# Trunk kernel, two layers: folded mean and epsilon, two other banks for the first values, a shifted start of x's transposition, and a last group in halves

## The chip, the cores and the metric

The kernel runs on one core of a Trainium2 chip. The metric is the time of one execution on the device in microseconds (us). Before the change it is 1112.16 us, the median of three runs (1112.07 to 1112.44). All engine times below come from one execution that the hardware profiler recorded.

## What is computed

A trunk of two layers runs over 512 tokens of width 1024, in float32. Layer 0 is multi-head latent attention with 8 heads and a block-causal mask; layer 1 is chunked attention with 16 heads, a learned position bias and a shared key/value band made from layer 0's output. Each layer ends in a SwiGLU FFN with hidden width 2816. Every sub-layer is x + post_norm(f(pre_norm(x))), and the norm is the place that one part of the change touches:

```python
EPS = 1e-6
def rms_norm(x, g):
    xf = x.astype(jnp.float32)
    y = xf * lax.rsqrt(jnp.mean(xf * xf, axis=-1, keepdims=True) + EPS)
    return (y * g.astype(jnp.float32)).astype(x.dtype)

def swiglu(h, w_gate, w_up, w_down):
    return (jax.nn.silu(h @ w_gate) * (h @ w_up)) @ w_down

def reference(x, ...):
    for layer in range(DEPTH):
        h = rms_norm(x, attn_pre_g[layer])
...
        x = x + rms_norm(y, attn_post_g[layer])
        h = rms_norm(x, ffn_pre_g[layer])
        f = swiglu(h, ffn_w_gate[layer], ffn_w_up[layer], ffn_w_down[layer])
        x = x + rms_norm(f, ffn_post_g[layer])
        if layer == N_A_LAYERS - 1:
            k_band, v_band = shared_kv(x, kv_src_g, w_kv_shared)
    return x
```

## The kernel before

**Layout.** Activations mostly lie transposed: a tile is 128 features by 512 tokens, so a [512, 1024] activation is eight tiles. Weights stream from memory. Every float32 factor is split into a high and a low part (`whi` by a cast on ScalarE, L144; `wlo` by a subtraction on VectorE, L145), and every product is three matmuls on TensorE: high by high, low by high, high by low (`mm3`, L360 to L364). The FFNs use a scheme of sums and differences of blocks with fewer products than the plain one, whose partial sums are called `al`, `be`, `ga`, `de`.

**Order.** The code is written as generators whose steps are woven into each other; a scheduler then orders the instructions of each engine's queue by priorities (`first`, `behind` and `issue_after` shift them). Each engine runs its queue strictly in order. PSUM has banks of 128 x 512 in three groups: "mm" (four), "s" (two), "t" (two). A matmul group that takes a bank waits until the former contents have been read.

**Norms.** `Sum` (L423) squares each tile on ScalarE and adds the squares up on VectorE in `acc`. `total` (L444) transposes `acc` on TensorE (`tot`) and reduces it on VectorE into `ss` (L452). `rstd` (L455) multiplies by 1/n and adds epsilon on VectorE (`v`, L463), and takes the power -1/2 on GpSimd (`r`, L467). `spread` (L484) brings `r` back over the partitions by matmuls with an identity (`bc`). In layer 0 the latents are computed from an x that isn't normalised, so their norms use `rstd_of_scaled` (L470), which also needs the first norm's `r`.

**Values and rotary part of layer 0.** `values_a(c)` (L928) makes the values of four token tiles, for the heads' first half (c = 0) or second half (c = 1): one bank and six matmuls per token tile, then the split `va` (L145, from ScalarE's cast of the same name). `rotary(0)` (L942) makes the queries' rotary part in two "s" banks (b_617 and b_618 before, b_613 and b_614 after); VectorE combines them (`ra`, `rb`, L949 to L951) and splits them (`rl`). The queries' norm is `tot_600`, `ss`, `v`, `r` and `r2` in between (L473 to L477).

**FFN.** `ffn()` (L1083) computes the input norm while the first products run, then `products()` (L1469) makes the hidden tiles in nine pairs of seven blocks each, and `down()` (L1235) multiplies them by the down weights. In the second FFN, `by_tokens` (L1164) runs beside the products as `aside`: block by block it loads a part of x, transposes it on VectorE (`xt`, L1171) and writes it to the output by four transfers on the SP queue, so that x stands in the output by tokens. It takes 24 steps, three per pair.

**The end.** `AfterLast` (L1403) finishes the last FFN's output, which lies by tokens: for token tile i and output half o it adds up the partial sums (`y`, L1322), squares with accumulation (`sq`, `ss`, L1327), multiplies by the gain (`yg`, L1442), forms mean and epsilon (`ssv`, L1364 and L1365) and the power on GpSimd (`r`, L1368). `plus_x` (L1461) then multiplies by `r`, adds x and issues the write. The last block of `down` (E6) works in groups of weight tiles; the last group is (3, 4, 5), its first output (e = 0) belongs to token tile 2 and its second (e = 1) to tile 3.

Of the kernel before, what the change touches and what calls it, by code (L numbers as in the profile page):

```python
# [68 lines left out]
def trunk(ctx: ExitStack, tc: tile.TileContext, a, out):  # L69
# [353 lines left out]
    class Sum:  # L423


        def __init__(self, make=U):
            self.make, self.acc, self.begun = make, None, [False, False]

        def add(self, src, h=None):
# [4 lines left out]
            if not self.begun[h or 0]:  # L434
                ins = nc.scalar.activation(self.acc[:, c], src, AF.Square),
            else:
                q = self.make(name="sq")
                ins = (nc.scalar.activation(q[:, c], src, AF.Square),
                       V.tensor_tensor(self.acc[:, c], self.acc[:, c], q[:, c], op=OP.add))
            for i in ((0, 1) if h is None else (h,)):  # L440
                self.begun[i] = True
# [13 lines left out]
    def rstd(ss, n, eps=EPS):  # L455
        parts = ss if isinstance(ss, list) else [ss]
        m = sum(p.shape[1] for p in parts)
        v = small("v")[:, :m]
        w = m // len(parts)
        for i, p in enumerate(parts):  # L460
            o = v[:, i * w:(i + 1) * w]
            if eps is EPS:
                V.tensor_scalar(o, p, 1.0 / n, EPS, op0=OP.mult, op1=OP.add)  # L463
            else:
                V.scalar_tensor_tensor(o, p, 1.0 / n, eps[:, i * w:(i + 1) * w], op0=OP.mult, op1=OP.add)
        r = small("r")[:, :m]
        nc.gpsimd.tensor_tensor(r, v, mhalf[:, :m], op=OP.pow)  # L467
        return r

    def rstd_of_scaled(ss, n, r0):  # L470
# [4 lines left out]
        r = rstd(v, n)  # L475
# [92 lines left out]
    class Post:  # L568
        def __init__(self, gain, make=U, eps=None, op=OP.add):

            self.gain, self.make, self.sum, self.y, self.r = gain, make, Sum(make), [], {}
            self.eps, self.op = eps, op

        def rstd(self, ss, h):
            return rstd(ss, D, EPS if self.eps is None else self.eps[:, 2 * h:2 * h + 2])
# [17 lines left out]
        def add_half(self, h, banks, rest, n1, n2, end=None):  # L593
# [7 lines left out]
            with behind(end and at):  # L601
                ss = self.sum.total(h, 200)
            with first(200):
                r = self.rstd(ss, h)
# [4 lines left out]
        def finish(self, b):  # L609
# [3 lines left out]
            for src in (self.sum.acc, sq):  # L613
                if src is sq:
                    nc.scalar.activation(sq[:, HALF[1]], b[:, HALF[1]], AF.Square)
# [4 lines left out]
            self.r[1] = spread(self.rstd([i[:, :1] for i in t], 1), 2)  # L620
# [216 lines left out]
    skv = Sum()  # L837
# [8 lines left out]
    r0 = rstd(sx.total(), D)  # L846
# [59 lines left out]
    sq_ = Sum()  # L906
# [176 lines left out]
    def ffn(i, x_src, osp, firsts, late=()):  # L1083
# [44 lines left out]
        ss = sx.sum.total()  # L1128
# [666 lines left out]
```

## Time and profile before

| quantity | value |
|---|---|
| median of three runs | 1112.16 us |
| lowest to highest | 1112.07 to 1112.44 us |
| the profiled execution's own time | 1113.16 us |
| its span from the first to the last instruction | 1111.4 us |
| granted TensorE clock, mean | 0.998 |
| GpSimd busy | 68.3 us, 106 instructions |
| memory traffic | 118 GB/s over the span |

In the profile, PE is TensorE, DVE VectorE, ACT ScalarE, POOL GpSimd and SP the queue that issues most transfers. A row of a timeline gives the start in us, the duration in us, the engine, the line of the code, the operation, what is written and read by the program's names, the shapes and a count; in brackets stands how long the engine had been idle and what ended that wait. `PE ... b<-whi,ckh` is a matmul into bank b. Matmuls overlap: a 128 x 512 one takes 0.39 us from start to end, but the next starts 0.23 us later, so a stop is read from the starts. Neighbouring operations of the other engines overlap by a little less than 0.1 us as well.

### The profile page before, as it was taken

What the parts mean: (1) busy time and instruction counts of PE and PEld (TensorE: products, weight loads), DVE (VectorE), ACT (ScalarE), POOL (GpSimd) and SP (SyncE); (2) the same over time, 40 slices, a digit from 0 to 9 for tenths busy, and PEclk for the clock granted to TensorE, in tenths of its full rate; (3) what the DMA queues carried; (4) which work ended last, traced back from release to release, by engine and by line L of the source; (5) the groups of instructions that cost most, each with busy time, mean ns of one, the idle gap of its engine ahead of it and who ended that gap; (6) DMA issues with size and microseconds to landing.
All of it is one profiled execution on the core that took longest, in us unless ns stands there. A gap on an engine that the chain in (4) does not pass through costs nothing.

```text
span 1111.4 us, 18953 instructions
## 1 busy us (share of the span) xinstructions
PE 1098.7 (99%) x6941; PEld 980.9 (88%) x6941; DVE 936.2 (84%) x1679; ACT 682.5 (61%) x1331; POOL 68.3 (6%) x106
## 2 busy tenths in 40 slices
PE   9999999999999999999999999999999999999997
PEld 6888889999999998888888888889999999998885
DVE  7788737999989989978868887758999999989977
ACT  6476636755555556668635777657755555556675
POOL 1200000000000001400000000000000000002402
PEclk9999999999999999999999999999999999999999
DMA  7432216323232357961556565635334444558913
GB/s 238 113 111 77 77 63 222 134 63 110 95 133 96 108 183 236 157 198 40 190 152 170 142 175 151 169 97 189 134 104 123 132 137 124 150 192 244 173 29 76
DMA packets 79885, 152.93 MB, mean 138 GB/s; under 512 B 25328, under 2 KB 27120, under 8 KB 79792
## 3 DMA queue, kind: packets, MB, share of 16 engines
q1 hardware_dynamic: 72448, 138.71, 40.2%
q0 software_dynamic: 6912, 12.59, 6.9%
q8 instruction: 54, 0.88, 0.3%
q10 hardware_dynamic: 432, 0.44, 0.1%
q14 instruction: 39, 0.32, 0.1%
HBM read 120.56 MB, written 10.68 MB: 118 GB/s over the span
## 4 chain that ended last, share of the span: by engine, by line
PE 90%; DVE 5%; DMA 2%; issue 2%; ACT 1%; POOL 0%; DVEq 0%; POOLq 0%; SPq 0%; ACTq 0%
PE al L1499 17%; PE b L361 11%; PE b L362 11%; PE b L363 11%; PE be L1499 8%; PE al L1255 8%; PE be L1255 5%; PE ga L1499 4%; PE de L1255 3%; PE ga L1255 3%; PE pt L523 2%; DVE wlo L145 2%; DMA x<-in_x 1%; DMA raw<-in_w_pair 1%; PE b L1655 1%
## 5 line engine op out<-in xcount | busy, mean ns | idle before, releaser
L144 ACT CAST whi<-raw 128x1024 fp32r<-128x1024 f32 (+3 forms) x224 | 225.2, 1007 | 199.0 <-PE al L1499 65.1
L145 DVE TENSOR_TENSOR wlo<-raw,whi 128x1024 fp32r<-128x1024 f32 (+3 forms) x224 | 260.2, 1164 | 44.8 <-ACT whi L144 43.7
L1499 PE MATMUL al<-th,whi 128*128 128x256 f32 x432 | 122.9, 285 | 0.5 <-DVE ut L1511 0.5
L1499 PE MATMUL al<-th,wlo 128*128 128x256 f32 x432 | 121.0, 281 | 0.3 <-DVE wlo L145 0.3
L1499 PE MATMUL al<-tl,whi 128*128 128x256 f32 x432 | 120.9, 280 | 0.0
L361 PE MATMUL b<-xh,whi 128*128 128x512 f32 (+1 forms) x298 | 114.6, 386 | 0.4 <-ACT whi L144 0.4
L363 PE MATMUL b<-xh,wlo 128*128 128x512 f32 (+1 forms) x298 | 110.3, 370 | 0.3 <-DVE wlo L145 0.3
L362 PE MATMUL b<-xl,whi 128*128 128x512 f32 (+1 forms) x298 | 109.9, 369 | 0.0
L174 DVE TENSOR_TENSOR raw<-raw,raw 128x1024 f32<-128x1024 f32 x72 | 86.9, 1218 | 2.5 <-DMA raw<-in_w_pair 2.2
L1499 PEld LDWEIGHTS al<-th,whi 128*128 128x128 f32 x432 | 81.3, 188 | 2.8 <-DVE ut L1511 0.9
L1499 PEld LDWEIGHTS al<-th,wlo 128*128 128x128 f32 x432 | 81.2, 188 | 0.6 <-DVE wlo L145 0.5
L1499 PEld LDWEIGHTS al<-tl,whi 128*128 128x128 f32 x432 | 81.3, 188 | 0.0
L511 ACT ACTIVATE p<-p,mn 128x128 f32<-128x128 f32 (+1 forms) x96 | 54.0, 562 | 39.3 <-DVE mn L509 38.4
L145 DVE TENSOR_TENSOR ptl<-pt,pth 128x128 fp32r<-128x128 f32 (+1 forms) x96 | 46.6, 486 | 29.4 <-ACT pth L144 23.7
L145 DVE TENSOR_TENSOR wlo<-wd,whi 128x512 fp32r<-128x512 f32 x86 | 56.3, 685 | 14.7 <-ACT whi L144 14.4
L363 PEld LDWEIGHTS b<-xh,wlo 128*128 128x128 f32 x298 | 56.2, 189 | 10.8 <-DVE wlo L145 1.2
L144 ACT CAST whi<-wd 128x512 fp32r<-128x512 f32 x86 | 49.8, 618 | 25.0 <-PE al L1255 10.7
L361 PEld LDWEIGHTS b<-xh,whi 128*128 128x128 f32 x298 | 56.5, 189 | 6.7 <-ACT whi L144 0.9
L362 PEld LDWEIGHTS b<-xl,whi 128*128 128x128 f32 x298 | 56.5, 190 | 5.8 <-DVE xl L149 0.2
L144 ACT CAST pth<-pt 128x128 fp32r<-128x128 f32 (+1 forms) x96 | 40.3, 421 | 26.8 <-PE pt L523 26.0
L1255 PE MATMUL al<-whi,pl 128*128 128x512 f32 x132 | 51.5, 390 | 0.0
L1255 PE MATMUL al<-whi,ph 128*128 128x512 f32 x132 | 51.4, 389 | 0.0
(313 smaller groups left out, 3266.8 us busy)
## 6 DMA issues: line engine op xcount, KB each, us to landing
raw<-in_w_pair SPq DMA_DIRECT2D x72, 512.0 KB, 3.8
wd<-in_w_down SPq DMA_DIRECT2D x54, 256.0 KB, 5.8
raw<-in_w_o SPq DMA_DIRECT2D x16, 512.0 KB, 3.6
raw<-in_w_gu SPq DMA_DIRECT2D x16, 512.0 KB, 4.2
raw<-in_w_down SPq DMA_DIRECT2D x16, 512.0 KB, 4.3
raw<-in_w_qkb SPq DMA_DIRECT2D x16, 512.0 KB, 3.5
wd<-in_w_down POOLq DMA_DIRECT2D x22, 256.0 KB, 5.2
wd<-raw POOLq DMA_DIRECT2D x22, 256.0 KB, 4.6
```

Source lines behind the costliest of these rows:

```text
L144: return (nc.scalar.copy(dst_hi, src), V.tensor_tensor(dst_lo, src, dst_hi.bitcast(F32), op=OP.subtract))
L145: V.tensor_tensor(dst_lo, src, dst_hi.bitcast(F32), op=OP.subtract))
L174: V.tensor_tensor(t, x, y, op=OP.add)
L361: nc.tensor.matmul(o, l[0], r[0], start=start, stop=False)
L362: nc.tensor.matmul(o, l[0], r[1], start=False, stop=False)
L363: last_mm[0] = nc.tensor.matmul(o, l[1], r[0], start=False, stop=stop)
L511: nc.scalar.activation(p[:, :n], p[:, :n], AF.Exp, bias=mn[:, :1], scale=-1.0, accum_out=self.sums[:, qt:qt + 1])
L523: nc.tensor.transpose(t[:, kt * P:(kt + 1) * P], p[:, kt * P:(kt + 1) * P], ident)
L1255: nc.tensor.matmul(to[e], l[c], r[d], start=j < 4 and k == 0 and n == 0, stop=k == NF // 2 - 1 and n == 2, skip_group_check=True)
L1499: nc.tensor.matmul(o, l[c], r[d], start=first_ and n == 0, stop=k == K2 - 1 and n == 2, skip_group_check=True)
L1655: nc.tensor.matmul(o[:, q_], vv, ptl[:, kt, q_], start=False, stop=kt == NQT - 1)
```

## The change

It has four parts.

1. *Mean and epsilon.* The squares are made with a scale of D^-0.5, so the sum is the mean already; the first addition of squares adds EPS/128 to each partition's share, which makes epsilon in the sum over 128 partitions. `rstd` is then the power alone. The two latents' norms keep the old form (`mean=False`), with the operation moved into `rstd_of_scaled`.
2. *Banks.* Of the first values (c = 0), token tiles 0 and 3 take an "s" bank each.
3. *x.* In `products`, the `aside` steps begin with the second pair (p = 1).
4. *The last group.* For e = 1 the group (3, 4, 5) runs in two halves of 256 columns: the first onto the old bank, the second in a fresh one of group "t" (`last`). What the old bank already held in the second half is added to `y` earlier (in `during`). `half` handles each half; the write for (0, 2) is issued behind that for (1, 2).

```diff
     class Sum:
-        def __init__(self, make=U):
-            self.make, self.acc, self.begun = make, None, [False, False]
+        def __init__(self, make=U, mean=True):
+            self.make, self.acc, self.begun, self.eps = make, None, [False, False], [mean, mean]
+            self.scale = D ** -0.5 if mean else 1.0
...
+                ins = nc.scalar.activation(q[:, c], src, AF.Square, scale=self.scale),
+                if self.eps[both[0]]:
+                    ins += V.scalar_tensor_tensor(t, t, EPS / P, q[:, c], op0=OP.add, op1=OP.add),
+                    for i in both:
+                        self.eps[i] = False
+                else:
+                    ins += V.tensor_tensor(t, t, q[:, c], op=OP.add),
...
-    def rstd(ss, n, eps=EPS):
-        parts = ss if isinstance(ss, list) else [ss]
...
-                V.tensor_scalar(o, p, 1.0 / n, EPS, op0=OP.mult, op1=OP.add)
...
+    def rstd(v):
+        r = small("r")[:, :v.shape[1]]
+        nc.gpsimd.tensor_tensor(r, v, mhalf[:, :v.shape[1]], op=OP.pow)
         return r
...
-        r = rstd(v, n)
+        V.tensor_scalar(v, v, 1.0 / n, EPS, op0=OP.mult, op1=OP.add)
+        r = rstd(v)
...
-    skv = Sum()
+    skv = Sum(mean=False)
...
-    sq_ = Sum()
+    sq_ = Sum(mean=False)
...
-            b = bank()
+            b = bank() if c or tt % 3 else bank("s")
...
-        V.tensor_scalar(eps, ss, EPS / D, EPS * EPS, op0=OP.mult, op1=OP.add)
+        V.tensor_scalar(eps, v, EPS, None, op0=OP.mult)
...
+                end = group[-1] == Down.TILES - 1
                 for e in range(2):
...
+                    for o, cols in post.parts(j, e, to[e]) if end else ((to[e], ALL),):
+                        fresh = o is not to[e]
...
+                                    nc.tensor.matmul(o[:, cols], l[c], r[d], start=begin and n == 0,
...
+                        if cols is not ALL:
+                            post.half(o, cols)
+                        elif end:
+                            post.one(j, e, o)
+                post.during(j, group[0], to)
...
+            if j == Down.E6 and i == 2:
+                t, c = self.y[0][3], HALF[1]
+                V.tensor_tensor(t[:, c], t[:, c], banks[1][:, c], op=OP.add)
...
+        def parts(self, j, e, b):
+            if j != Down.E6 or not e:
+                return (b, ALL),
+            return (b, HALF[0]), (bank("t", "last"), HALF[1])
+
+        def half(self, b, c):
+
+            t, v, q = self.y[0][3], self.v[:, 3:4], HALF.index(c)
+            with first(200):
+                V.tensor_tensor(t[:, c], t[:, c], b[:, c], op=OP.add)
+                sq = U(name="sq")
+                nc.scalar.activation(sq[:, c], t[:, c], AF.Square, accum_out=self.ends[:, q:q + 1])
+                if not q:
+                    self.yg = U(name="yg")
+                    V.scalar_tensor_tensor(v, self.ss[1][:, 3:4], 1.0 / D, self.eps[:, 3:4], op0=OP.mult, op1=OP.add)
+                V.tensor_tensor(self.yg[:, c], t[:, c], self.g[0][:, c], op=OP.mult)
+                self.summed = V.scalar_tensor_tensor(v, self.ends[:, q:q + 1], 1.0 / D, v, op0=OP.mult, op1=OP.add)
+                if q:
+                    self.y[0][3] = self.yg
+                    self.r[3] = small("r")[:, :1]
+                    nc.gpsimd.tensor_tensor(self.r[3], v, mhalf[:, :1], op=OP.pow)
...
                 if i == 2:
                     self.plus_x(1, 2, nc.sync)
+                    self.plus_x(0, 2, nc.scalar)
...
             with tc.issue_after(self.summed.ins):
-                self.plus_x(0, 2, nc.scalar)
                 self.plus_x(1, 3, nc.sync)
...
-                if aside is not None and j in (1, 3, 5):
+                if aside is not None and p and j in (1, 3, 5):
                     next(aside, None)
```

The built programs show how the queues change. First VectorE in the first FFN's input norm, before and after (`wlo` is the low part of a weight, `acc` the sum of the output norm of the attention, `bc` the spread factor):

```order
L145 TENSOR_TENSOR wlo_2349<-raw_2209,whi_2348 128x1024
L439 TENSOR_TENSOR acc_1940<-acc_1940,sq_2078 128x256
L452 TENSOR_REDUCE ss_2115<-tot_2112 128x2
L145 TENSOR_TENSOR wlo_2388<-raw_2303,whi_2387 128x1024
L463 TENSOR_SCALAR v_2117<-ss_2115 128x2
L439 TENSOR_TENSOR acc_1940<-acc_1940,sq_2147 128x256
```
```order
L145 TENSOR_TENSOR wlo_2341<-raw_2203,whi_2340 128x1024
L447 TENSOR_TENSOR acc_1936<-acc_1936,sq_2074 128x256
L460 TENSOR_REDUCE ss_2111<-tot_2108 128x2
L145 TENSOR_TENSOR wlo_2380<-raw_2297,whi_2379 128x1024
L447 TENSOR_TENSOR acc_1936<-acc_1936,sq_2141 128x256
```

`v` is gone from its place behind the `wlo`; the reduction's result goes to GpSimd directly.

Second, VectorE between the rotary products and the second values of layer 0 (`v` and `r` belong to the queries' norm, b_617/b_618 and b_613/b_614 are the rotary banks, `va` reads a bank of the second values), before and after:

```order
L950 TENSOR_TENSOR rb_644<-b_618,sin_406 128x512
L473 TENSOR_TENSOR v_131_607<-ss_605,r_356 128x4
L145 TENSOR_TENSOR wlo_732<-raw_625,whi_731 128x640
L474 TENSOR_TENSOR v_131_607<-v_131_607,r_356 128x4
L951 TENSOR_TENSOR ra_643<-ra_643,rb_644 128x512
L463 TENSOR_SCALAR v_610<-v_131_607 128x4
L145 TENSOR_TENSOR wlo_772<-raw_695,whi_771 128x640
L477 TENSOR_TENSOR r_134_614<-r_612,r_356 128x4
L145 TENSOR_TENSOR rl_649<-ra_643,rh_648 128x512
L1015 TENSOR_SCALAR nsq<-r_134_614 128x4
L145 TENSOR_TENSOR va_543<-b_720,va_543 128x512
```
```order
L473 TENSOR_SCALAR v_129_604<-v_129_604 128x4
L145 TENSOR_TENSOR wlo_728<-raw_621,whi_727 128x640
L476 TENSOR_TENSOR r_131_610<-r_608,r_354 128x4
L950 TENSOR_TENSOR ra_639<-ra_639,rb_640 128x512
L1014 TENSOR_SCALAR nsq<-r_131_610 128x4
L145 TENSOR_TENSOR rl_645<-ra_639,rh_644 128x512
L948 TENSOR_TENSOR ra_648<-b_613,sin_403 128x512
L949 TENSOR_TENSOR rb_649<-b_614,cos_404 128x512
L145 TENSOR_TENSOR wlo_768<-raw_691,whi_767 128x640
L145 TENSOR_TENSOR va_540<-b_716,va_540 128x512
```

The product with GpSimd's power (`r_134_614` before, `r_131_610` after, called `r2` in the code) now stands ahead of the combination `ra` and the split `rl`, and the second rotary pair stands ahead of the first second-half value `va`.

Third, VectorE in the tail (`be` and `last` are banks of the last group, `xt` is x by tokens), before and after:

```order
L1322 TENSOR_TENSOR y_12516<-y_12516,al_11901 128x512
L145 TENSOR_TENSOR wlo_12887<-wd_12139,whi_12886 128x512
L1442 TENSOR_TENSOR yg_12884<-y_12516,g_11936 128x512
L1364 SCALAR_TENSOR_TENSOR ssv_11899<-ss_1_11898,eps_9408 128x1
L1322 TENSOR_TENSOR y_12631<-y_12631,be_11904 128x512
L1442 TENSOR_TENSOR yg_12908<-y_12631,g_11934 128x512
L1365 SCALAR_TENSOR_TENSOR ssv_11899<-ss_1_11897,ssv_11899 128x1
L1466 SCALAR_TENSOR_TENSOR yg_12879<-yg_12879,r_12912,xt_12477 128x512
L1322 TENSOR_TENSOR y_12642<-y_12642,be_11905 128x512
```
```order
L145 TENSOR_TENSOR wlo_12871<-wd_12122,whi_12870 128x512
L1328 TENSOR_TENSOR y_12614<-y_12614,be_11887 128x512
L1454 TENSOR_TENSOR y_12625<-y_12625,be_11888 128x256
L1478 TENSOR_TENSOR yg_12892<-y_12614,g_11917 128x512
L1374 SCALAR_TENSOR_TENSOR ssv_11881<-ss_1_11879,ssv_11881 128x1
L1460 TENSOR_TENSOR yg_12921<-y_12625,g_11917 128x256
L1501 SCALAR_TENSOR_TENSOR yg_12862<-yg_12862,r_12896,xt_12460 128x512
L1501 SCALAR_TENSOR_TENSOR yg_12892<-yg_12892,r_12896,xt_12459 128x512
L1461 SCALAR_TENSOR_TENSOR ssv_11881<-ends,ssv_11881 128x1
L1454 TENSOR_TENSOR y_12625<-y_12625,last_12902 128x256
```

The addition of the last part of the last token tile (`y<-be` before, `y<-last` after) stood behind one `plus_x` (L1466) and now stands behind two (L1501). In the changed program the low part `wlo` of the last weight also stands behind an addition of 256 columns (`y<-be`, L1428), `yg` and `ssv`.

More of the change, by code (lines that the diff above doesn't have):

```diff
@@ L433, in add @@
                 self.acc = self.make(name="acc")
-            if not self.begun[h or 0]:
-                ins = nc.scalar.activation(self.acc[:, c], src, AF.Square),
+            t = self.acc[:, c]
+            both = (0, 1) if h is None else (h,)
+            if not self.begun[both[0]]:
+                ins = nc.scalar.activation(t, src, AF.Square, scale=self.scale),
             else:
                 q = self.make(name="sq")
-                ins = (nc.scalar.activation(q[:, c], src, AF.Square),
-                       V.tensor_tensor(self.acc[:, c], self.acc[:, c], q[:, c], op=OP.add))
-            for i in ((0, 1) if h is None else (h,)):
+                ins = nc.scalar.activation(q[:, c], src, AF.Square, scale=self.scale),
[5 more added lines that the diff above has]
+                    ins += V.tensor_tensor(t, t, q[:, c], op=OP.add),
+            for i in both:
                 self.begun[i] = True
@@ L453, in total @@
             return r
-    def rstd(ss, n, eps=EPS):
-        parts = ss if isinstance(ss, list) else [ss]
[L457 to L467, printed above, removed]
+    def rstd(v):
+        r = small("r")[:, :v.shape[1]]
+        nc.gpsimd.tensor_tensor(r, v, mhalf[:, :v.shape[1]], op=OP.pow)
         return r
@@ L568, in trunk, with __init__ @@
     class Post:
-        def __init__(self, gain, make=U, eps=None, op=OP.add):
+        def __init__(self, gain, make=U, op=OP.add):
             self.gain, self.make, self.sum, self.y, self.r = gain, make, Sum(make), [], {}
-            self.eps, self.op = eps, op
-        def rstd(self, ss, h):
-            return rstd(ss, D, EPS if self.eps is None else self.eps[:, 2 * h:2 * h + 2])
+            self.op = op
         def keep(self, b, k, c):
@@ L614, in finish @@
                 if src is sq:
-                    nc.scalar.activation(sq[:, HALF[1]], b[:, HALF[1]], AF.Square)
+                    nc.scalar.activation(sq[:, HALF[1]], b[:, HALF[1]], AF.Square, scale=self.sum.scale)
                 for i in range(2):
@@ L619, in finish @@
             self.keep(b[:, HALF[1]], KT - 1, HALF[1])
-            self.r[1] = spread(self.rstd([i[:, :1] for i in t], 1), 2)
+            v = small("v")[:, :2]
+            for i in range(2):
+                V.tensor_copy(v[:, i:i + 1], t[i][:, :1])
+            self.r[1] = spread(rstd(v), 2)
         def apply(self, x, h, each, to=None):
```

37 lines of the change are left out of this document (19 added, 18 removed).

## The prediction

> **What bounds the kernel now.** I read the page first (busy time of the engines, the chain that ended last), then the matmuls' starts against their usual spacing, and then the timelines of the five places that the change touches.
>
> ```profile
> PE 1098.7 (99%) x6941; PEld 980.9 (88%) x6941; DVE 936.2 (84%) x1679; ACT 682.5 (61%) x1331; POOL 68.3 (6%) x106
> ...
> PE 90%; DVE 5%; DMA 2%; issue 2%; ACT 1%; POOL 0%; DVEq 0%; POOLq 0%; SPq 0%; ACTq 0%
> ```
>
> TensorE is busy 1098.7 of 1111.4 us, and 90% of the chain is its own. The number of matmul products does not fall. So nothing that DVE, ACT or POOL save is worth anything unless PE stood still for it, or it lies in the tail behind the last matmul. What the change can gain is only a few stops of PE, each under 1.2 us, and the tail of some 7 us. The sum below goes place by place against the profiled execution: 1113.16 us, of which the span is 1111.4. The timed median is 1112.16, so I take changes of the span over to the median as they are. A difference of about 0.2%, 2.2 us, is what a measurement of this kernel can tell from no change.
>
> **Mean and epsilon in the squares.** Seven small operations `v` go, each 0.16 us on DVE; the first addition in each sum becomes a scalar_tensor_tensor instead of a tensor_tensor. DVE's busy time hardly moves. What counts is where `v` stood: behind a 1024-wide `wlo`. In the second FFN's input norm DVE, POOL and PE show:
>
> ```profile
> 762.65 0.42 DVE L452 TENSOR_REDUCE ss<-tot 128x2 f32<-128x256 f32 x1
> 762.99 1.22 DVE L145 TENSOR_TENSOR wlo<-raw,whi 128x1024 fp32r<-128x1024 f32 x1
> 764.12 0.16 DVE L463 TENSOR_SCALAR v<-ss 128x2 f32<-128x2 f32 x1
> 764.29 0.43 DVE L439 TENSOR_TENSOR acc<-acc,sq 128x256 f32<-128x256 f32 x1
> ```
> ```profile
> 764.43 0.84 POOL L467 TENSOR_TENSOR r<-v,mhalf 128x2 f32<-128x2 f32 x1 [52.62 <-DVE v L463]
> ```
> ```profile
> 764.03 0.28 PE L361 MATMUL b<-oh,wh 128*128 128x256 f32 x1
> 764.15 0.28 PE L362 MATMUL b<-ol,wh 128*128 128x256 f32 x1
> 765.33 0.43 PE L484 MATMUL bc<-ident,r 128*128 128x128 f32 x2 [0.90 <-POOL r L467]
> ```
>
> 256-wide matmuls start 0.12 apart, so PE lost 765.33 - 764.15 - 0.12 = 1.06 us here. After the change the power `r` may start when the reduction is done, 763.07 plus the 0.15 that lay between `v`'s end and `r`'s start, 763.22. But then the `wlo` of 762.99 to 764.21 is running, and powers that meet such work take longer. One power shows how much:
>
> ```profile
> 27.91 2.07 POOL L467 TENSOR_TENSOR r<-v,mhalf 128x4 f32<-128x4 f32 x1 [13.13 <-DVE v L463]
> ```
> ```profile
> 28.14 0.95 DVE L145 TENSOR_TENSOR wlo<-raw,whi 128x768 fp32r<-128x768 f32 x1
> ```
>
> It ended at 29.98, 0.89 after that `wlo`, while the same shape in a gap of DVE took 1.01 (the row at 55.28 below). So the power waits for DVE operations that read two tensors of SBUF, and then takes nearly its whole time. In the second FFN it would end either near 764.07 + 0.70 = 764.77, or, if the addition right behind `wlo` takes its turn first, near 765.2. `bc` also stands two matmuls earlier on PE now, so 0.24 us of work moves behind the stop. The gain is 0.32 or minus 0.1; I take 0.1, between them, with 1.06 and -0.2 as bounds.
>
> The Trainium skill, "SBUF — State Buffer", section "SBUF: two separate sides", says that GpSimd and a VectorE operation with two SBUF inputs lock a shared port pair against each other, for the whole instruction, whoever starts first. By that rule the power would start at 764.21 and end at 764.91, a gain of 0.18 in place of my 0.1; the sum would move by 0.08. The trace agrees that they exclude each other, but at 27.91 the power's record starts 0.23 before the `wlo` that held it, so the start in the record is not what decides.
>
> The first FFN has the same place with a shorter stop:
>
> ```profile
> 182.11 1.22 DVE L145 TENSOR_TENSOR wlo<-raw,whi 128x1024 fp32r<-128x1024 f32 x1
> 183.25 0.16 DVE L463 TENSOR_SCALAR v<-ss 128x2 f32<-128x2 f32 x1
> ```
> ```profile
> 183.90 0.28 PE L363 MATMUL b<-oh,wh 128*128 128x256 f32 x1
> 184.31 0.43 PE L484 MATMUL bc<-ident,r 128*128 128x128 f32 x2
> ```
>
> PE lost 184.31 - 183.90 - 0.12 = 0.29. Here `bc` keeps its place, no addition follows `wlo` closely, and the power would end near 183.33 + 0.70 = 184.03, about when PE comes. I take all 0.29 (0 to 0.29). The other norms cost PE nothing I can gain. Sum of this part: **-0.4** (from -1.4 to +0.2).
>
> **First values in two other banks.** Before, PE stops twice in the second values, where b_744 and b_753 reuse the bank of the value two before, as only two of four banks turn (the head's q and k hold the others):
>
> ```profile
> 57.49 0.39 PE L363 MATMUL b<-whi,ckl 128*128 128x512 f32 x1
> 58.00 0.50 PE L361 MATMUL b<-whi,ckh 128*128 128x512 f32 x1
> ...
> 59.26 0.40 PE L363 MATMUL b<-whi,ckl 128*128 128x512 f32 x1
> 59.79 0.51 PE L361 MATMUL b<-whi,ckh 128*128 128x512 f32 x1
> ```
> ```profile
> 55.04 0.16 DVE L463 TENSOR_SCALAR v<-v 128x4 f32<-128x4 f32 x1
> 55.77 0.82 DVE L145 TENSOR_TENSOR wlo<-raw,whi 128x640 fp32r<-128x640 f32 x1 [0.57 <-ACT whi L144]
> ...
> 57.26 0.68 DVE L145 TENSOR_TENSOR va<-b,va 128x512 fp32r<-128x512 f32 x1
> ```
> ```profile
> 55.28 1.01 POOL L467 TENSOR_TENSOR r<-v,mhalf 128x4 f32<-128x4 f32 x1 [8.24 <-DVE v L463]
> ```
>
> 512-wide matmuls start 0.23 apart: 0.28 and 0.30 lost, with the slower restarts (0.34 to the next one) about 0.8 in all. b_744 starts at 58.00, when the `va` of 57.26 is done. The new banks serve the *first* values only; the second ones still turn in two, so these waits stay, and what decides is when DVE reads the second values. The order of the changed kernel has, on DVE: `wlo`, then `r2` (waits for the power), `ra`+`rb`, `nsq`, `rl`, `ra`, `rb`, `wlo`, `va`. The transposes for the query norm now come before the rotary products, so `v` is ready near 52.9 instead of 55.20; `wlo` of that moment runs till 53.6 and holds the power, which ends near 54.5. `r2` follows, and behind it in DVE's queue everything else waits, with one step through ACT (`rh`, 0.6): 0.07 + 0.68 + 0.7 (ACT and handover) + 0.6 + 0.6 + 0.6 (`rl`, `ra`, `rb`: 0.68 each, less the 0.08 by which neighbours on DVE overlap, as 763.07 and 762.99 above) + 0.75 (`wlo`) + 0.68 (`va`) = 4.7, so `va` is read at 59.2. PE would be there at 57.6: a stop of 1.6 in place of 0.28. The next value finds its bank free; head 1's q (b_758) waits some 0.3 for the third `va`. Together 1.6 + 0.3 + two slow restarts 0.2, less 0.8: **+1.2**. Below: all waits gone, -0.8. Above: the power takes 2.07 as at 27.91, +2.2. I stay with the walk.
>
> **x turned from the second pair on.** In the first pair of the second FFN the transposition of x stood ahead of what PE waited for:
>
> ```profile
> 823.67 0.71 DVE L1171 STREAM_TRANSPOSE xt<-x 128x512 f32<-128x512 f32 x1
> ...
> 825.41 2.35 DVE L145 TENSOR_TENSOR wlo<-raw,whi 128x1024 fp32r<-128x1024 f32 x2
> ```
> ```profile
> 826.07 0.28 PE L1499 MATMUL al<-tl,whi 128*128 128x256 f32 x1
> 826.68 0.39 PE L1499 MATMUL al<-th,wlo 128*128 128x256 f32 x1 [0.33 <-DVE wlo L145]
> ```
>
> PE lost 826.68 - 826.07 - 0.12 = 0.49, and 0.1 in the restart. Without `xt`, 0.63 to the next start on DVE, `wlo` is there in time. The eighth block's transposition and its four writes move to pair 8, past the loads on SP:
>
> ```profile
> 991.87 1.87 SPq L220 DMA_DIRECT2D wd<-in_w_down x4
> ...
> 993.23 1.23 DVE L145 TENSOR_TENSOR wlo<-raw,whi 128x1024 fp32r<-128x1024 f32 x1 [0.54 <-ACT whi L144]
> ```
>
> DVE is idle there (0.54 before this row, with more around it), which covers most of the 0.63. The four writes put the loads back by some four times 0.47 us, but what they load is used by the down products, more than 15 us later; without that cover it would be 1.9. I take **-0.55** (from -0.6 to 0).
>
> **Last group in two halves.** 15 matmuls of 512 become 30 of 256: 30 x 0.118 - 15 x 0.227 = 0.1 on PE. The tail before:
>
> ```profile
> 1099.15 0.68 DVE L145 TENSOR_TENSOR wlo<-wd,whi 128x512 fp32r<-128x512 f32 x1
> ...
> 1100.66 0.69 DVE L1322 TENSOR_TENSOR y<-y,be 128x512 f32<-128x512 f32 x1 [0.16 <-PE be L1255]
> ...
> 1102.99 0.75 DVE L1466 SCALAR_TENSOR_TENSOR yg<-yg,r,xt 128x512 f32<-128x512 f32 x1 [0.69 <-POOL r L1368]
> 1104.11 0.69 DVE L1322 TENSOR_TENSOR y<-y,be 128x512 f32<-128x512 f32 x1 [0.36 <-PE be L1255]
> ...
> 1105.66 0.74 DVE L1466 SCALAR_TENSOR_TENSOR yg<-yg,r,xt 128x512 f32<-128x512 f32 x1
> 1106.86 1.54 DVE L1466 SCALAR_TENSOR_TENSOR yg<-yg,r,xt 128x512 f32<-128x512 f32 x3 [0.45 <-POOL r L1368]
> ```
> ```profile
> 1102.39 0.57 POOL L1368 TENSOR_TENSOR r<-ssv,mhalf 128x1 f32<-128x1 f32 x1 [3.11 <-DVE ssv L1365]
> 1105.83 1.00 POOL L1368 TENSOR_TENSOR r<-ssv,mhalf 128x1 f32<-128x1 f32 x1 [2.87 <-DVE ssv L1365]
> ```
> ```profile
> 1104.83 0.63 ACT L1327 ACTIVATE sq<-y 128x512 f32<-128x512 f32 x1 [2.72 <-DVE y L1322]
> ```
>
> Now `wlo` stands behind a half-width addition, `yg` and `ssv`, and comes at 1100.84; PE does nine half products meanwhile and stops some 0.2, so the sum for output half 0 is ready at 1101.65, a full microsecond later than 1100.63. From there on DVE: addition (to 1102.35), first half's addition (1102.8), `yg` 512, `ssv` (1103.46), power on POOL with a 256-wide `yg` in flight (to 1104.2), and then **two** `plus_x` (to 1105.7) that stand ahead of the second half's addition. PE has the second half ready at 1104.10, as before, but it is added only at 1105.67: 1.56 later than the row at 1104.11. Halving gives part back: addition 0.43 in place of 0.69, Square about 0.4 in place of 0.63, and the last power 0.57 in place of 1.00, since no `plus_x` runs beside it. That is 1105.67 + 0.43 + 0.4 + 0.2 (reading the sum) + 0.25 (`ssv`, handover) + 0.57 + handovers = 1107.5 for the last `plus_x` chain, against 1106.86. **+0.65**. If the addition came when PE is ready, it would be -0.9; with a held power, +1.1. What follows (1.54 on DVE, DMA, closing, 4.5 in all) stays.
>
> **Sum.** -0.4 + 1.2 - 0.55 + 0.65 = +0.9: 1113.1 us, and a span of 1112.3 in a profile like the one read.
>
> **Rivals.** *The waits go as drawn*: the second values find banks free (-0.8) and the second half is added when PE has it (-0.9), with the whole of the first part (-1.4) and the third: -3.7, 1108.5 us. Against it stand the two-bank turn and the order on DVE, which are fixed in the program. *The banks only*: the power is early enough and the second values' stops merely vanish: -0.4 - 0.8 - 0.55 + 0.65, 1111.1 us; the earlier transposes speak for it, the stop of DVE at `r2` against it. *Slower*: in the first head two `wlo` now stand on DVE ahead of its `ql` and `kl`. The scores' low products need `kl`; on my walk it is ready at 66.6 and PE comes at 67.6. If the conversions on ACT or their loads are over 1 us later, PE stands behind both:
>
> ```profile
> 67.60 0.95 DVE L145 TENSOR_TENSOR wlo<-raw,whi 128x768 fp32r<-128x768 f32 x1
> ```
>
> That and a 640-wide one (0.82) are 1.8 us: 1114.9. For it: DVE is full in this stretch; against it: the slack, and that the scores stand later on PE now.
>
> **How the numbers follow.** Forecast 0.60, banks only 0.16, all waits gone 0.12, slower 0.12. The first two lie within 2.2 us of 1112.16: same 0.76, faster 0.12, slower 0.12. The bounds of the parts add up to -3.8 and +3.5 or more; they will not all fall on one side. The range from 1110.3 to 1114.9 takes in the forecast, the banks case and most of the slower one, and leaves out most of the faster.
>
> **What would show it.** Right: PE's stop before the third second value grows above 1 us, behind `va`, with `r2` on DVE waiting for POOL near 53 to 54.5; the stop before `bc` near 184 is gone, that near 765 stays close to 1 us; no stop at 826; in the tail the second half's addition starts right after two `plus_x`, over 1 us after the last matmul, and the last power takes about 0.6. Wrong: second values without a stop, a power that runs beside `wlo` in 0.7, an addition that starts with PE's end, or new stops of PE at the first scores.

## The result and the profile after

| quantity | before | after |
|---|---|---|
| median of five runs each, us | 1112.44 (1112.07 to 1114.14) | 1117.33 (1116.47 to 1118.58) |
| ratio, with its 95% interval | 1 | 1.0041 (1.0026 to 1.0055) |
| profiled execution: own time, us | 1113.16 | 1116.47 |
| its span, us | 1111.4 | 1114.7 |
| last matmul's start to the end of the span, us | 7.70 | 8.17 |

The change makes the kernel slower by 0.41%, 4.6 us; the two medians lie 4.9 us apart. The forecast was 1113.1 with a range up to 1114.9, so the time lies above the range. The profiled execution before is 0.7 us above its median and the one after 0.9 below, so the two traces differ by only 3.3 us; the account below is of that difference. One execution of the run e1 below, of 3646.74 us, was in a slow state and is left out of its time.

The page of the changed kernel, engines and chain:

```profile
PE 1099.5 (99%) x6956; PEld 982.8 (88%) x6956; DVE 937.8 (84%) x1675; ACT 681.9 (61%) x1333; POOL 70.0 (6%) x106
...
PE 88%; DVE 4%; DMA 3%; issue 2%; ACT 1%; SPq 1%; POOL 0%; DVEq 0%; POOLq 0%; ACTq 0%
```

TensorE's work grew by 0.8 us only, and the chain has two points less of it. So TensorE stood still for longer. The view of waits names where. It gives, for TensorE in the changed kernel, the waiting operation and its line, the one that released it, and the us in total, the times and the longest:

```profile
PE b L361 <- DVE va L145: 1.5, 1, 1.5
...
PE tot L457 <- DVE acc L447: 0.9, 1, 0.9
...
PE bc L483 <- POOL r L465: 0.6, 1, 0.6
PE sc L1046 <- ACT kh L144: 0.5, 1, 0.5
PE al L1534 <- DVE ut L1546: 0.4, 1, 0.4
```

The same view before has none of the rows `va`, `acc` and `kh`. I then matched the two programs' matmuls one by one and read how late each of after starts against its partner of before:

| stretch (us of before) | after is later by, at its end | gained or lost there |
|---|---|---|
| up to 43 | -0.08 | -0.08 |
| 43 to 72 (first values to first scores) | 3.78 | **+3.86** |
| 72 to 802 | 2.40 | -1.38 |
| 802 to 858 (x, first pair) | 1.88 | -0.5 |
| 858 to 990 | 2.02 | +0.1 |
| 990 to 1005 (x, last pair) | 2.63 | +0.6 |
| the tail, to the end | 3.3 | +0.65 |

The loss lies in 29 us near the start. The limits are places where both kernels have the same matmuls behind them. In between the order differs: at 44 two matmuls of the queries stand earlier, which makes their neighbours 0.45 later without any stop. Of the -1.38, 0.34 lies at the first FFN's norm, 0.29 at the second's and 0.20 at one more norm near 801. Another 0.84 are two short stops at 272 and 292 that TensorE had in the trace of before and not, or only in part, in that of after; some 0.3 comes back bit by bit. Nothing that the change touches is near these two, and the traces of e5 and e6, which are the kernel before with an edit elsewhere, don't have them or only a part of them, so I put them to differences from run to run.

**Three stops in the new banks' stretch.** The timeline of after around the first one, TensorE, VectorE and GpSimd:

```profile
47.08 0.39 PE L363 MATMUL b<-whi,ckl 128*128 128x512 f32 x1
48.42 0.30 PE L457 MATMUL tot<-ident,acc 128*128 128x128 f32 x1 [0.95 <-DVE acc L447]
```
```profile
44.06 0.81 DVE L145 TENSOR_TENSOR wlo<-raw,whi 128x640 fp32r<-128x640 f32 x1
44.79 3.48 DVE L447 TENSOR_TENSOR acc<-acc,sq 128x512 f32<-128x512 f32 x2
```
```profile
44.05 1.98 POOL L1018 TENSOR_TENSOR sik<-kr,sik 64x512 f32<-64x512 f32 x1 [0.32 <-DMA sik<-rot]
46.10 1.62 POOL L1020 TENSOR_TENSOR kr<-kr,sik 64x512 f32<-64x512 f32 x1
```

512-wide matmuls start 0.23 apart, so TensorE lost 48.42 - 47.08 - 0.23 = 1.11. It waits for the last two additions of squares for the queries' norm. VectorE has them begun in time, but the pair takes 3.48 us, and beside it run two of GpSimd's three products for the rotary part of the keys. In before these three products ran at 42.73, 44.38 and 45.75, while VectorE read PSUM or stood idle:

```profile
44.13 0.69 DVE L145 TENSOR_TENSOR va<-b,va 128x512 fp32r<-128x512 f32 x1 [2.03 <-ACT va L144]
44.73 0.74 DVE L149 SCALAR_TENSOR_TENSOR cql<-b,gains,cqh 128x512 fp32r<-128x512 f32 x1
45.78 0.75 DVE L149 SCALAR_TENSOR_TENSOR cql<-b,gains,cqh 128x512 fp32r<-128x512 f32 x1 [0.31 <-ACT cqh L148]
```
```profile
44.38 1.29 POOL L1019 TENSOR_TENSOR sik<-kr,sik 64x512 f32<-64x512 f32 x1 [0.37 <-DMA sik<-rot]
```

There nobody was held: 0.69 to 0.75 on VectorE, 1.28 to 1.30 on GpSimd. The free banks let the queries' squares come earlier, and so into GpSimd's products.

The second stop is the one that was forecast. TensorE, VectorE and GpSimd of after:

```profile
58.60 0.39 PE L363 MATMUL b<-whi,ckl 128*128 128x512 f32 x1
60.48 0.50 PE L361 MATMUL b<-whi,ckh 128*128 128x512 f32 x1 [1.50 <-DVE va L145]
```
```profile
55.76 0.16 DVE L476 TENSOR_TENSOR r<-r,r 128x4 f32<-128x4 f32 x1 [0.91 <-POOL r L465]
...
59.02 0.81 DVE L145 TENSOR_TENSOR wlo<-raw,whi 128x640 fp32r<-128x640 f32 x1
59.75 0.68 DVE L145 TENSOR_TENSOR va<-b,va 128x512 fp32r<-128x512 f32 x1
```
```profile
54.20 1.52 POOL L465 TENSOR_TENSOR r<-v,mhalf 128x4 f32<-128x4 f32 x1 [6.49 <-DVE v L473]
```

60.48 - 58.60 - 0.23 = 1.65, behind the walk of the prediction: the power, VectorE idle for 0.91 before `r2`, and eight operations from `r2` to `va`.

The third stop stands before the first scores. TensorE and ScalarE of after:

```profile
67.64 0.39 PE L363 MATMUL b<-cqh,wlo 128*128 128x512 f32 x1
68.58 0.50 PE L1046 MATMUL sc<-kh,qh 128*128 128x128 f32 x2 [0.55 <-ACT kh L144]
```
```profile
67.21 0.84 ACT L144 CAST whi<-raw 128x768 fp32r<-128x768 f32 x1 [1.94 <-issue]
67.95 0.58 ACT L144 CAST kh<-b 128x512 fp32r<-128x512 f32 x1
```

0.71 is lost. With slow restarts and a short stop behind it (0.2 at 71.16), the delay against before grows by 1.28 from 63 to 72 us. The scores need `kh`, the high part of the keys. On ScalarE `kh` stands behind the conversion of a weight, and ScalarE was idle for 1.94 before that conversion. In before `kh` stood ahead of the conversions:

```profile
63.25 0.59 ACT L144 CAST kh<-b 128x512 fp32r<-128x512 f32 x1
63.74 0.73 ACT L144 CAST whi<-raw 128x640 fp32r<-128x640 f32 x1
```

The profile names no releaser for the idle time of 1.94 ("issue"). TensorE's last read of an earlier converted weight (`b<-ckl,whi`) ended at 67.13, just ahead of it; that this was the buffer which the conversion writes is inferred from these times.

**The other parts.** The powers of the FFNs' input norms, and TensorE's stop in the second:

```profile
186.05 1.60 POOL L465 TENSOR_TENSOR r<-ss,mhalf 128x2 f32<-128x2 f32 x1 [130.33 <-DVE ss L460]
...
766.02 1.54 POOL L465 TENSOR_TENSOR r<-ss,mhalf 128x2 f32<-128x2 f32 x1 [51.25 <-DVE ss L460]
```
```profile
765.80 1.22 DVE L145 TENSOR_TENSOR wlo<-raw,whi 128x1024 fp32r<-128x1024 f32 x1
```
```profile
766.73 0.28 PE L363 MATMUL b<-oh,wh 128*128 128x256 f32 x1
767.62 0.43 PE L483 MATMUL bc<-ident,r 128*128 128x128 f32 x2 [0.61 <-POOL r L465]
```

The stop is 0.77 in place of 1.06. The power ends at 767.56, 0.54 after the `wlo` that runs beside it. In the last pair of the second FFN, VectorE and TensorE:

```profile
993.98 0.71 DVE L1170 STREAM_TRANSPOSE xt<-x 128x512 f32<-128x512 f32 x1 [0.49 <-DMA x<-mid]
994.61 0.72 DVE L1546 TENSOR_TENSOR ut<-al,ut 128x256 f32<-128x256 f32 x2
```
```profile
995.05 0.39 PE L1534 MATMUL al<-th,whi 128*128 128x256 f32 x1 [0.36 <-DVE ut L1546]
```

The transposition waits for its own load and stands ahead of the `ut` that frees TensorE's bank. And in the tail, VectorE:

```profile
1106.95 1.41 DVE L1501 SCALAR_TENSOR_TENSOR yg<-yg,r,xt 128x512 f32<-128x512 f32 x2 [0.47 <-POOL r L1377]
1108.28 0.15 DVE L1461 SCALAR_TENSOR_TENSOR ssv<-ends,ssv 128x1 f32<-128x1 f32 x1
1108.35 0.41 DVE L1454 TENSOR_TENSOR y<-y,last 128x256 f32<-128x256 f32 x1
...
1110.16 1.54 DVE L1501 SCALAR_TENSOR_TENSOR yg<-yg,r,xt 128x512 f32<-128x512 f32 x3 [0.67 <-POOL r L1465]
```

The second half's addition starts at 1108.35 behind two `plus_x`, 1.54 after TensorE's last matmul has ended (1106.81).

### The profile page after: what moved, and what is told of

The parts are those of the page before. It is cut to its first block, busy times and chain, and to the rows that moved or that the text cites. A ratio compares the mean times of both kernels' runs of the same rounds, so it can differ in the third digit from the quotient of the medians.

```text
span 1114.7 us, 18982 instructions
## 1 busy us (share of the span) xinstructions
PE 1099.5 (99%) x6956; PEld 982.8 (88%) x6956; DVE 937.8 (84%) x1675; ACT 681.9 (61%) x1333; POOL 70.0 (6%) x106
## 4 chain that ended last, share of the span: by engine, by line
PE 88%; DVE 4%; DMA 3%; issue 2%; ACT 1%; SPq 1%; POOL 0%; DVEq 0%; POOLq 0%; ACTq 0%
PE al L1534 18%; PE b L361 10%; PE b L362 10%; PE b L363 10%; PE be L1534 9%; PE al L1259 8%; PE be L1259 5%; PE ga L1534 4%; PE de L1259 3%; PE ga L1259 3%; PE pt L522 2%; DVE wlo L145 1%; PE b L1690 1%; PE b L1689 1%; PE sc L1682 1%
```

## The experiments

Twelve kernels were run. Their ratios are against the kernel before on the same chip, whose median in these sessions was 1112.26 to 1112.82. The labels are those that the expectations use.

### The banks alone, and all but the banks (e1_banks_only, e2_banks_undone)

```diff
-            b = bank()
+            b = bank() if c or tt % 3 else bank("s")
```

Alone in the kernel before (e1), and taken back in the changed kernel (e2).

> The kernel before with the second part alone (token tiles 0 and 3 of the first values in two 's' banks). Theory: this part costs nearly all that the changed kernel lost: three stops of TensorE, about 1.1 us before the transposes of the queries' norm near 48, 1.7 before the third of the second values near 60, 0.9 before the first scores near 68, less the 0.8 of stops that go. Span longer than before by 3.3 to 3.9 us. Rival: the loss comes from several parts together, and this part alone costs what the prediction said, 1.2 us (0.8 to 1.6).

> The changed kernel without the second part (all first values in 'mm' banks again). Theory: the other three parts together are worth -0.5 (norms) + 0.1 (x: 0.5 gained in the first pair, 0.6 lost in the last) + 0.65 (tail) = about +0.3 us against the kernel before (-0.5 to +1.0). Rival: the other parts carry a good part of the loss, over +1.5 us.

Banks alone: 1117.23 (four executions), ratio 1.0044 (1.0028 to 1.0060). Its matmuls are 0.37 late at 43 and 4.27 at 72, so 3.9 is lost in the stretch, with the same stops: 1.11 before the totals, 1.66 behind `va`, 0.71 before the scores; the pair of additions takes 3.47. All but the banks: 1113.2, ratio 1.0006 (0.9997 to 1.0016), with the two stops of 0.28 in the second values as before. So the banks carry the loss, and the other three parts together are worth something between -0.3 and +1.8 us.

### GpSimd's key products moved (e3_key_late)

In the changed kernel, the three products go behind the queries' power on GpSimd. The other engines keep their order.

```diff
-        nc.gpsimd.tensor_tensor(sik[:64], kr[64:], sik[64:], op=OP.mult)
-        nc.gpsimd.tensor_tensor(kr[:64], kr[:64], cos[:64], op=OP.mult)
-        nc.gpsimd.tensor_tensor(kr[:64], kr[:64], sik[:64], op=OP.add)
+        with tc.issue_after(powers[-1].ins):
+            nc.gpsimd.tensor_tensor(sik[:64], kr[64:], sik[64:], op=OP.mult)
+            nc.gpsimd.tensor_tensor(kr[:64], kr[:64], cos[:64], op=OP.mult)
+            nc.gpsimd.tensor_tensor(kr[:64], kr[:64], sik[:64], op=OP.add)
```

> The changed kernel with GpSimd's three products of the rotary key put behind the power of the queries' norm in GpSimd's own queue; the order on every other engine is the same. Theory: the two additions of the query squares take 3.48 us in the changed kernel because they read two tensors of SBUF while GpSimd's products (42.4 to 47.7) do too. Now they take 1.3 to 1.4, and the stop of 1.1 before the transposes near 48 goes. The key's products then run from about 54.5 to 58.5 beside VectorE's ra, rl, rb and wlo and hold some of these, 0.6 to 2 us, in front of the second values, so the span gains between 1.1 and -0.5. Rival: the additions wait for ScalarE's squares or for something else; they still take about 3.5 and the stop stays.

VectorE and GpSimd in this run:

```profile
46.14 1.48 DVE L447 TENSOR_TENSOR acc<-acc,sq 128x512 f32<-128x512 f32 x2
...
55.87 1.80 DVE L952 TENSOR_TENSOR ra<-ra,rb 128x512 f32<-128x512 f32 x1
57.59 1.26 DVE L1016 TENSOR_SCALAR nsq<-r 128x4 f32<-128x4 f32 x1
```
```profile
55.83 1.29 POOL L1021 TENSOR_TENSOR sik<-kr,sik 64x512 f32<-64x512 f32 x1
57.20 1.62 POOL L1022 TENSOR_TENSOR kr<-kr,cos 64x512 f32<-64x512 f32 x1
```

The same pair of additions takes 1.48 in place of 3.48, and TensorE's stop before the totals is gone. Where the products now run, `ra` takes 1.80 in place of 0.68 and `nsq` 1.26 in place of 0.16; both stand ahead of `va`, and the stop there grows from 1.65 to 62.03 - 58.64 - 0.23 = 3.16. The mechanism is shown in both directions. Against the changed kernel the matmuls gain 1.3 by 52 us and lose 1.5 again by 60, so the edit costs 0.2 there, within what was expected. The time is 1120.35, ratio 1.0076 (1.0061 to 1.0091), 3.0 above the changed kernel's, and this stretch does not explain that. The trace has 1.4 us more at 22 us than the changed kernel's, a stop of the start that varies between runs, and 0.6 more between 250 and 300, where the edit changes no operation; the rest stays open.

The Trainium skill, "SBUF — State Buffer", section "SBUF: two separate sides", says that a VectorE operation with two SBUF inputs and a GpSimd operation that reads SBUF exclude each other: the one that starts first holds the shared ports for the whole instruction, and the other is blocked. The stretched additions and `ra`, both with two SBUF inputs, agree with it: each grew by about one GpSimd product (1.0 to 1.1 of 1.29).

### ScalarE's keys ahead of the weights (e4_kh_ahead)

```diff
             if k == 2:
-                feed.ahead()
+                with tc.issue_after(halves[-1].ins) if h == 1 else nullcontext():
+                    feed.ahead()
...
-        split(kh, kl, bk)
+        halves.extend(split(kh, kl, bk)[:1])
```

> The changed kernel with the conversions of three later weights put behind the first head's kh in ScalarE's queue (the scheduler then also moves their wlo on VectorE). Theory: the first scores wait near 68 because kh stands behind a conversion that waits for TensorE to finish the second head's k; now the stop of 0.9 there goes, and that of 1.7 before the third second value falls by 0.75, as one wlo no longer stands ahead of its read. Span shorter than the changed kernel's by 1.3 to 1.7 us. Rival: the scores wait for the rotary queries' transfers on SP; then the stop stays and only about 0.7 is gained.

1114.95, ratio 1.0032 (1.0018 to 1.0047). TensorE comes to the first scores without a stop:

```profile
65.72 0.40 PE L363 MATMUL b<-ckh,wlo 128*128 128x512 f32 x1
65.96 0.39 PE L1049 MATMUL sc<-kh,qh 128*128 128x128 f32 x2
```

The stop behind `va` shrank as well, to 59.21 - 58.05 - 0.23 = 0.93: the edit also moves these weights' `wlo` on VectorE, so that one less stands ahead of `va`. Against the changed kernel the matmuls are 0.5 early at 22 and 2.5 early at 72, so the stretch gained 2.0.

### r2 out of the way, and both queue edits (e9_factor_late, e11_queues_mended)

```diff
-        rq = rstd_of_scaled(sq_.total(), QL, r0)
+        return rstd_of_scaled(sq_.total(), QL, r0, True)
...
+        with tc.issue_after(lows[-1].ins):
+            query_factor(power)
```

`query_factor` makes `r2` and `nsq`; `lows` holds the splits `rl`. In e11 the edit of e4 is there too.

> The changed kernel, with two of VectorE's steps for the mean moved behind the second r x l product: r2 (which waits for GpSimd's power) and nsq. The other engines' order is the changed kernel's. Theory (r2 holds up the conversion va that TensorE waits for): the 1.66 us stop before b_740 falls by the 0.9 to 1.1 us for which r2 stood idle and computed, to about 0.6; the stops before the totals' transposes (1.1) and before the first scores (0.7 and its small followers) stay; span 0.9 to 1.1 below the changed kernel's 1114.7. Rival (va is bound by what stands behind it on another engine, or by its own input): the stop stays within 0.3 of 1.66 and the span within 0.3.

> The changed kernel with both queue edits: ScalarE's three weight conversions behind kh, and VectorE's r2 and nsq behind the second r x l product. Theory: of the three stops of the new banks only the one before the totals' transposes (1.1 us) is left, so the time is 2.3 to 2.7 us below the changed kernel (about 1114.8), and about 1 above the kernel with the banks undone (1113.2 beside a before of 1112.5). Rival (the two edits shorten the same wait): no more than 0.3 below the run with kh ahead alone (ratio 1.0032).

TensorE in e9:

```profile
58.27 0.39 PE L363 MATMUL b<-whi,ckl 128*128 128x512 f32 x1
59.10 0.50 PE L361 MATMUL b<-whi,ckh 128*128 128x512 f32 x1 [0.44 <-DVE va L145]
```

The stop is 0.60 where 1.65 was, as expected: 1.05 of it came from `r2` and the short `nsq`. 1.1 is gained in the stretch, the other two stops stay. 1115.56, ratio 1.0027 (1.0018 to 1.0037). But the span is 1116.0, not below 1114.7, since the profiled execution gave the gain back elsewhere: 0.8 bit by bit between 855 and 895, and 1.5 in the last pair. In the first of these its matmuls start 0.1200 apart in place of 0.1173, at a granted clock of 1.00 in both traces. The trace of e5 has the same slower stretch without this edit; its cause I did not find. The last pair:

```profile
995.25 0.71 DVE L1180 STREAM_TRANSPOSE xt<-x 128x512 f32<-128x512 f32 x1 [2.06 <-DMA x<-mid]
```

With both edits: 1115.45, ratio 1.0025 (1.0015 to 1.0035), 1.9 below the changed kernel where 2.3 to 2.7 was expected. The stop before the totals is left (1.05), the one behind `va` is 0.58, but the next one, before head 1's q, grew from 0.28 to 0.68. The intervals of e4, e9 and e11 overlap: the run cannot say by medians how far the two edits add. In the last pair this run's trace lost 1.4 us more than the changed kernel's, too.

### x two steps later (e5_x_two_later)

In the kernel before, the steps of x begin inside the first pair, at its last place, rather than with the second pair.

```diff
-                if aside is not None and j in (1, 3, 5):
+                if aside is not None and j in ((1, 3, 5) if p else (5,)):
```

> The kernel before with x's steps begun two steps later instead of three (in the first pair only the last slot is used). Theory: the third part of the change gains 0.5 to 0.6 us in the first pair and gives 0.6 back in the last, because the last transposition stands on VectorE ahead of ut and waits there for its own load of x. With the load in the pair before, the last transposition finds its data, and the stop in the last pair stays under 0.2; span shorter than before by 0.3 to 0.5 us. Rival: the last pair is slow because of the transposition's own 0.63 us on VectorE; then it costs 0.4 to 0.6 there again, and the sum is about zero.

1111.62, ratio 0.9988 (0.9978 to 0.9997). The stops of the first pair are gone and the last pair has none: the last transposition stands there at 985.23 and does not wait. So both ends can be had. By medians this is 1.2 below before, more than the 0.3 to 0.5 expected, and the trace can't price the edit: of what it gains, 1.2 lies in the start and 1.0 near 272 and 292, beside 0.65 in the first pair, and 1.0 is given back bit by bit between 858 and 920.

### The second values in the t banks (e6_second_t)

```diff
-            b = bank()
+            b = bank("t") if c and tt > 1 else bank()
```

> The kernel before with token tiles 2 and 3 of the SECOND values in the two 't' banks. Theory: the two stops of 0.28 and 0.30 with their slow restarts come from the second values turning in two 'mm' banks; here both go, and nothing else moves ahead of them: 0.7 to 0.8 us shorter before the first scores. Rival: the next matmuls (the second head's q) wait for the same reads instead, and the time stays within 0.3 of before.

1112.59, ratio 0.9998 (0.9989 to 1.0007). The two stops in the second values go, and by 62 us 0.85 is gained. Then TensorE stands before the first scores, which it did not do before; TensorE and ScalarE:

```profile
63.28 0.39 PE L363 MATMUL b<-ckh,wlo 128*128 128x512 f32 x1
64.07 0.50 PE L1047 MATMUL sc<-kh,qh 128*128 128x128 f32 x2 [0.40 <-ACT kh L144]
```
```profile
62.81 0.73 ACT L144 CAST whi<-raw 128x640 fp32r<-128x640 f32 x1
63.43 0.59 ACT L144 CAST kh<-b 128x512 fp32r<-128x512 f32 x1
```

0.56 is lost to the same queue as in the changed kernel, 0.66 with the slow restarts. So 0.2 stays in the trace where 0.7 to 0.8 was expected, less than the medians can tell.

### The additions of the tail ahead (e7_tail_late)

From e2, with both `plus_x` of token tile 2 put behind the second half's sum.

```diff
-                if i == 2:
-                    self.plus_x(1, 2, nc.sync)
-                    self.plus_x(0, 2, nc.scalar)
...
             with tc.issue_after(self.summed.ins):
+                self.plus_x(1, 2, nc.sync)
+                self.plus_x(0, 2, nc.scalar)
                 self.plus_x(1, 3, nc.sync)
```

> The changed kernel with the second part undone, and with both plus_x of token tile 2 behind the last half's sum on VectorE. Theory: the last half's addition waits 1.5 us behind these two; now it starts with TensorE's end, and the time from the last matmul's start to the end of the span is 0.6 to 0.8 shorter than with banks undone alone. Rival: the power on GpSimd is then held by the two plus_x beside it, takes 1.0 to 2.0 instead of 0.55, and the tail gains less than 0.3.

VectorE and GpSimd in the tail of this run, whose last matmul starts at 1102.53:

```profile
1102.84 0.42 DVE L1454 TENSOR_TENSOR y<-y,last 128x256 f32<-128x256 f32 x1 [0.29 <-PE last L1259]
...
1103.93 2.87 DVE L1500 SCALAR_TENSOR_TENSOR yg<-yg,r,xt 128x512 f32<-128x512 f32 x5
```
```profile
1104.08 1.02 POOL L1465 TENSOR_TENSOR r<-ssv,mhalf 128x1 f32<-128x1 f32 x1 [1.17 <-DVE ssv L1461]
```

The addition now starts as TensorE's last matmul ends. From the last matmul's start to the end the kernel takes 7.32 us, against 8.16 in e2 and 7.70 in the kernel before; this though the last power takes 1.02 beside a `plus_x` in place of 0.55. 1112.8, ratio 0.9997 (0.9988 to 1.0006), where e2 has 1.0006 (0.9997 to 1.0016).

### The parts put together (e8_mended, e10_whole_tail, e12_norms_and_x)

e8 has the first part of the change, x as in e5, the t banks of e6 and the tail of e7. In e10 the last group is whole, as before. e12 has the first part and x of e5 alone.

> The parts that should help, together: mean and epsilon in the squares (-0.5), x's steps two slots later (-0.4), the second values' last two tiles in 't' banks (-0.75), the last group in halves with both plus_x of tile 2 late (-0.1). Theory: 1.5 to 2 us below the kernel before, about 1110.5. Rival: some of the parts meet the same waits again and the sum stays within 0.5 us of before.

> The kernel of e8_mended (mean with the squares, x two steps later, second values in the t banks) with the last group whole, as before the change. Theory (halving the last group costs 0.65 as changed and gives about 0.2 with both additions out of the way): within 0 to 0.3 us above e8_mended (ratio 0.9985), about 1.5 below before. Rival (the halves cost even then): faster than e8_mended by 0.3 or more.

> The kernel before with two parts alone: the mean with the squares, and x turned two steps later; the values keep the banks of before and the last group is whole. Theory: the stops of the first pair (0.49 and 0.1) and part of those at the first layers (0.4) go and none comes at the last pair: 0.9 to 1.1 us below before (ratio 0.9990 to 0.9992), and within 0.6 us of e10_whole_tail. Rival (the second values' banks carried the gain of e8_mended): within 0.3 us of before.

| run | time, us | ratio (95% interval) | last matmul's start to the end, us |
|---|---|---|---|
| e8_mended | 1110.88 | 0.9985 (0.9977 to 0.9994) | 7.33 |
| e10_whole_tail | 1110.59 | 0.9980 (0.9972 to 0.9988) | 7.71 |
| e12_norms_and_x | 1111.74 | 0.9989 (0.9980 to 0.9997) | 7.70 |

All three are faster than the kernel before, by 1.1 to 2.2 us; for e12 the interval ends just below 1. Whether e8 or e10 is faster isn't settled, since their intervals overlap: e10 was expected 0 to 0.3 above e8, and its median is 0.3 below. Their traces give the halves 0.2 us: 0.39 in the tail, less the 0.17 that TensorE loses among the narrower matmuls. e12 came out as expected against before, but 1.15 above e10 where at most 0.6 was expected. The t banks do not account for it: from 43 to 72 us they are worth 0.2 in the traces of e8 and e10, as in e6. Most of what e12's trace loses against e10's comes bit by bit between 72 and 450 (1.4), where the two kernels don't differ; its profiled execution shows a granted clock of 0.947 in place of 0.999, so this comparison is weak.

## Why the prediction was wrong

**The step that failed** is the second term of the sum, the two other banks: +1.2 forecast, +3.9 in the trace. Of its walk, the part that was written down held. The stop behind `va` was forecast at 1.6 and is 1.65, by the reason given (e9: without `r2` in the way, 0.60); the one before head 1's q was to be 0.3 and is 0.28. The recorded sum of these places, 1.6 + 0.3 + 0.2 - 0.8, makes 1.3 rather than 1.2; in the trace they cost 1.39. That the size held is in part luck: TensorE came to this stop at 58.8 and `va` was ready at 60.4, both 1.2 later than walked, because the first stop, which the walk did not have, held the matmuls and the totals alike. What is missing are two stops, 2.5 together with their restarts, that the walk did not reach:

- *1.11 before the totals (1.19 with the restart).* The prediction let the transposes for the query norm come earlier and took that as a gain for `v`. It did not ask what the additions ahead of these transposes would run beside. It had the very rule at hand, for the power, and used it for that alone; GpSimd's three key products, the only other GpSimd work in that stretch, were never placed against VectorE's new order. e3 shows the cause.
- *0.71 before the first scores (1.28 with what follows it).* The prediction named new stops there as a sign of being wrong, and it is the place of the rival "slower", but not its mechanism: it had `kl` wait on VectorE behind two `wlo`, for 1.8; what came is `kh` on ScalarE behind one conversion. The prediction walked VectorE's queue to the scores and gave a slack of 1.0 there, and took ScalarE's queue only as a condition of that rival. e4 puts `kh` ahead of the conversions, and the stop goes. (It moves these weights' `wlo` on VectorE too, but the profile names `kh` on ScalarE as what ended the wait.)

The rival's condition, conversions on ScalarE over 1 us late, is close to what came: ScalarE stood idle for 1.94 before this one. Its chance of 0.12 was too low for a term whose own sum was walked on one engine out of three. The bounds of that term (-0.8 to +2.2) were too narrow for the same reason.

**The mean and epsilon** were right in kind and gave more than forecast: 0.8 in the trace, where the sum had 0.4. (Eight of the operations `v` went, by the rows of L463; the prediction counted seven.) There is no stop near 184, which gains 0.34 where 0.29 was forecast, and 0.77 in place of 1.06 near 765, which gains 0.29. The power there ends 0.54 after `wlo`, as in the first of the two cases of the prediction (0.56). The forecast took 0.1, between the two cases, 0.32 and -0.1. These gains are recorded 0.06 too high: they leave out the time from the power's end (765.27) to `bc` (765.33) in before. The 0.20 near 801 was not foreseen: the prediction said that the other norms cost TensorE nothing to gain.

**x** was right at the first pair (-0.5 against -0.55) and wrong at the last, where the cost was set to nothing with VectorE's idle time as cover. The idle time is there (0.49 in the row at 993.98), but it is the transposition itself that waits, for its own load, and it stands ahead of `ut`. It cost 0.6 in the trace of after; the stop there was 0.4 to 2.05 in the seven traces of kernels that have this part. So the third part lies anywhere from about -0.1 to +1.5, and e5 shows that it need not cost anything.

**The last group** was right to the size: +0.65 forecast and found, behind two `plus_x` as told (0.47 of it behind the last matmul's start, the rest among TensorE's matmuls of the group). e7 takes the wait behind the two `plus_x` out.

**What stays open.** The medians differ by 1.6 us more than the two traces (4.9 and 3.3). The stops of the start and of the last pair vary by as much from run to run: against the changed kernel's trace, those of e3, e4, e9 and e11 lie from 0.75 earlier to 1.36 later at 25 us. But no trace of another execution of the changed kernel is there to show it. That the conversion on ScalarE waited for its buffer is read from the times (67.13 and 67.21), and was not tried with another buffer.

## What to carry to other kernels

A freed bank does not only take away the wait for it: it lets other work come earlier, and what that work then runs beside has to be walked on every engine, GpSimd included, up to the next place where TensorE could stand. Ahead of a transposition that waits for a load, or of a conversion whose buffer is still read, put what TensorE waits for. Where one term is walked on one engine only, its upper bound should hold a stop for each queue that was not walked.

## What the runs showed of the hardware

VectorE's operations with two inputs in SBUF and GpSimd's products stretch each other in both directions. A pair of additions took 3.48 beside two products and 1.48 without; the products took 1.98 and 1.62 in place of 1.29. That a 128 x 4 `nsq` with one tensor input took 1.26 in place of 0.16 beside GpSimd was not expected either. Beside VectorE's operations that read one of their inputs from PSUM, neither engine was slowed (0.69 to 0.75, and 1.28 to 1.30).
